# A three-layer transformer stack in one kernel: the first norm's scale vector transposed and applied after the transpose, instead of broadcast

## The chip, the cores and the metric

One core of one Trainium2 chip runs the whole kernel in one launch. TensorE (PE) multiplies, ScalarE (ACT), VectorE (DVE) and GpSimd (POOL) do the rest, SyncE (SP) issues most of the loads over 16 DMA engines. The metric is the device time of one execution in microseconds (us), as the median of several runs.

## What is computed

The input `x` has 256 tokens of 1024 features, in float32. Two blocks follow each other. The first has two layers, each a norm, an attention mixer and a feed-forward part; the second has one layer with a gated feed-forward part ahead of its mixer and one behind. Every matrix product is made in float32 accuracy out of a high and a low part of each operand. What the change touches is the very first step, the norm ahead of the first mixer, whose result is multiplied by the mixer's weights:

```
def rmsnorm(x, g):
    xf = x.astype(jnp.float32)
    y = xf * lax.rsqrt(jnp.mean(xf * xf, axis=-1, keepdims=True) + RMS_EPS)
    return (y * g.astype(jnp.float32)).astype(x.dtype)

hn = rmsnorm(h, mix_norm[layer])        # layer 0: h is x
h = h + moba_nsa_mixer(hn, ...)         # begins with hn @ w_in
```

## The kernel before

The 256 tokens are two token tiles of 128 (index t), the 1024 features eight k tiles of 128. Products want the features on the partitions, so a normed token tile (`xn`, [128 tokens, 1024]) is transposed by TensorE, 128 columns at a time, four k tiles to a PSUM bank. The helper `turn` (L389) does this: four transposes into one bank, then `split` (L385), one ACT copy of [128, 512] into the rounded part `hi` and one DVE subtraction of [128, 512] that leaves the rest, `lo`. Both go to the tile `xx` ([128, 8 k tiles, 512]: `hi` of 256 tokens, then `lo` of 256).

The weights come as a stream of chunks (class `Stream`). SP loads a chunk into `raw`; ACT and DVE split it into `whi` and `wlo` in pieces; `pump` (L96) emits the next piece that is due. The first two chunks are small ([128, 1120], four k tiles of 280 columns each); the first of them is loaded and split in two halves of 560 columns.

`setup` (L523) issues the first loads on SP's queue in this order: `x` of token tile 0 in two halves, the scale vector `mix_norm[0]` broadcast to all 128 partitions (`gain`, L148, by `load_bc`, L144: 128 copies of 4 KB), the identity (part of `cst`), the two halves of the first chunk, `x` of token tile 1, the second chunk, the small tables `rel_bias` and `oh`, the rest of `cst`. It also has PE multiply zeros `WARM` = 4 times, [128, 128] by [128, 384], ahead of anything useful; the trace shows two records for each.

`start_norm` (L583) emits, in this order: the norm of tile 0 (`prenorm`, L430), one split piece, the turn of tile 0 (two banks), one split piece, the norm of tile 1, one split piece (the second chunk). A norm is `squares` (L405, two ACT passes with sums), `ms` on DVE (L422), a power on POOL (L415), and two DVE products `xn = x * r * gain` of [128, 512] (`scaled`, L425). The turn of tile 1 is kept in `late_turn` and emitted later, by `begin` (L315), raised in priority by `soon(300)` over the 300 instructions emitted before it.

`setup`, `start_norm` and `rel_tables` (L561, the table of relative biases, which has one PE product, a DVE copy into S and a trip through memory on POOL's queue) stand inside `tc.manual_schedule()` (L1503). What comes after, from `even` (L598) on, is ordered by the framework's own scheduler. The waits between engines are put in by the framework.

`even` begins with `begin`: for token tile 0, then tile 1, the product with the first two chunks, 8 k tiles by 3 products (hi by hi, hi by lo, lo by hi) of 280 columns, so 24 for each tile. Behind it come products of 256 columns that need `xx` of both token tiles (`projB`, L219; in the trace `ps_p<-xx,whi`).

Of the kernel before, what the change touches and what calls it, by code (L numbers as in the profile page):

```python
# [15 lines left out]
BIG = 1e30  # L16
# [5 lines left out]
WARM = 4  # L22
# [12 lines left out]
class Stream:  # L35
    """The weights in the order of their use: DMA -> raw, raw -> hi (ScalarE) and lo = raw - hi (VectorE)."""
# [26 lines left out]
    def piece(self):  # L63
        """Emits half a chunk's split; False where its buffers or its data aren't due yet."""
        if self.prepped >= len(self.split):
            return False
        j = self.prepped
        c = self.split[j]
        if c.raw is None or (not c.spare and c.ring >= RING and not self.ring[c.ring - RING].done):
            return False  # L70
        K, nc = self.K, self.K.nc
        if c.hi is None:
            if c.spare:
                both = K.t([128, 4096], "T16", 1, F32R)
                c.hi, c.lo = both[:, :2048], both[:, 2048:]
            elif c.n == 128:
                both = K.t([128, 2048], "whi", RING, F32R)
                c.hi, c.lo = (both[:, :256].rearrange("p (k a n) -> p k a n", k=8, a=2)[:, :, i] for i in range(2))
                c.both = both[:, :256].rearrange("p (k n) -> p k n", k=8)
            else:  # L80
                c.hi = K.t([128, 2048], "whi", RING, F32R)
                c.lo = K.t([128, 2048], "wlo", RING, F32R)
        a, b = c.at, (c.n if c.n - c.at <= 1200 else c.at + 1024)
        if not j and not a:
            b = c.n // 2
        if c.n == 128:
            K.split(c.hi, c.lo, c.raw[:, :128].rearrange("p (k n) -> p k n", k=8))
        else:
            K.split(c.hi[:, a:b], c.lo[:, a:b], c.raw[:, a:b])
        c.at = b  # L90
        if b == c.n:
            self.prepped += 1
            self.load()
        return True
# [19 lines left out]
class Kern:  # L114
# [12 lines left out]
    def soon(self, n):  # L127
        """What is emitted inside comes before the n instructions emitted last, where it can."""
        return self.tc.high_priority(offset=n)

    def later(self, inst, than):
        """inst comes after than in their engine's order."""
        self.tc.add_manual_dep(getattr(inst, "ins", inst), getattr(than, "ins", than).name, mybir.DependencyInfo(
            mybir.DependencyClass.NoSync, mybir.DependencyReason.DATA), reason="order")
# [80 lines left out]
    def mmo(self, out, l, r, start):  # L215
        """One start in a bank: later products write or add, column by column, as those stand."""
        self.nc.tensor.matmul(out, l, r, start=start, stop=False, skip_group_check=True)  # L217

    def projB(self, c, f, ps, xx, w=256, quantum=4, one=True):  # L219
        """Features f of chunk c, feature-major: ps[:, :256] = W^T x^T, or the sum of ps's halves where not one."""  # L220
# [15 lines left out]
    def addB(self, ps, dst):  # L236
        """dst = left half + right half of a projB result."""
# [9 lines left out]
    def chunkB(self, xx, evac):  # L247
        """One chunk of 256 features; evac(f, ps)."""
# [13 lines left out]
    def smallB(self, xx, evac):  # L262
        """[128 tokens, 2, 16] product with the chunk of 16 features, for evac, by way of the feature-major
        one: (W_hi | W_lo)^T x_hi and W_hi^T x_lo, whose parts the turn adds."""
# [20 lines left out]
    def projA(self, c, out, xx, k0, nk, n, start, stop, T=(0, 1)):  # L285
        """out[t] ([128 tokens, n]) += x[t] W, nk k tiles from k0."""
# [11 lines left out]
    def chunkA(self, xx, n, evac, ready=None):  # L298
        """Two chunks of 4 k tiles, n columns, token-major; evac(t, ps), once ready()."""
# [15 lines left out]
    def begin(self, xx, items):  # L315
        """The start of a layer, token-major, token tile 0 before tile 1 is there.  items: (n, evac) for n
        columns in two chunks of 4 k tiles, or (256, evac) for a chunk of 256 features; evac(t, ps) may
        return what is to follow once tile 1's products are under way."""
# [29 lines left out]
    def flush(self):  # L348
        """Emits what waits for the next products to be under way."""
# [3 lines left out]
    def feature_major(self, evac, func=AF.Copy, tag="b"):  # L353
        """An item of begin() whose features go to evac(f, ps) as from chunkB."""
# [15 lines left out]
    def down(self, c, acc, hx, k0, start, stop, T=(0, 1)):  # L370
        """acc[t][half] += h[t] W, the two k tiles of c ([2, 1024])."""
# [17 lines left out]
    def turn(self, src, xx, k0, t, n=4, tag="b", than=None):  # L389
        """xx[:, k0:k0+n, token tile t] = hi and lo of the transposed src ([128 tokens, n * 128]); not before  # L390
        the product than."""
# [13 lines left out]
    def squares(self, halves, junk):  # L405
        """Two parts of mean(x^2) of 1024 columns given in two halves"""
# [11 lines left out]
    def rstd(self, halves, junk, eps):  # L418
        """(mean(x^2) + eps)^-1/2 of 1024 columns given in two halves"""
# [19 lines left out]
    def attend(self, jobs):  # L439
        """Causal softmax attention, one job a head: ready(), qk = [(q, k) feature-major] (one or two  # L440
        maps, q times minus its scale), T() = minus the bias with +BIG where masked ([128, 128] for
        query tile 0, [128, 256] for 1), v, O() and col.  Scores, transposes and products with v of
        a head are two and three steps apart."""
# [79 lines left out]
    def setup(self):  # L523
# [13 lines left out]
        self.G0 = self.gain("mix_norm", 0, nc.sync)  # L537
        nc.sync.dma_start(c[:, 0:128], A["cst"][:, 0:128])
        self.ws.load(1)
# [21 lines left out]
    def rel_tables(self):  # L561
        """T[p, h, 255 - j] = -bias_h(128 + p - j), +BIG where that distance is negative."""
# [15 lines left out]
    def back(self, ap):  # L578
        """ap with its last dimension from the end."""
# [3 lines left out]
    def start_norm(self, eps):  # L583
        xx = self.xx = self.t([128, 8, 512], "xx", 2, F32R)
        a = self.prenorm(0, self.G0, eps)
        self.ws.pump(1)
        self.turn(a, xx, 0, 0, 8)
        self.ws.pump(1)
        b = self.prenorm(1, self.G0, eps)
        self.ws.pump(1)  # L590

        def late():
            with self.soon(300):
                self.turn(b, xx, 0, 1, 8, "p")
        self.late_turn = late

# [264 lines left out]
    def early_out(self, F, flag, oT, ks):  # L861
        """First k tiles of an output projection, token tile 0, while attention still runs."""
# [11 lines left out]
    def late_out(self, rest, epi, nlate=2):  # L874
        """The rest of an output projection: rest = (source, k) for each chunk that follows the early ones."""
# [74 lines left out]
    def post_epi(self, f, Gp, G, eps, out=None):  # L950
        """x += f norm(acc) Gp, and its prenorm or the end."""
# [108 lines left out]
    def log1pexp(self, z, n):  # L1060
        """log(1 + e) with e = exp(-|z|), z [128, n]: 2 artanh(t), t = e / (2 + e) <= 1/3, by its series to t^15."""
# [134 lines left out]
    def mixer2(self):  # L1196
# [182 lines left out]
        def ssm_end(g):  # L1379
            """sz is twice z's silu."""  # L1380
# [152 lines left out]
def _cols(w, n):  # L1533
    """[1024, N] -> chunks of n columns, [N / n, 128, 8 * n]"""
# [4 lines left out]
def _halves(w):  # L1539
    """[1024, 512 * m] -> [2 m, 128, 4 * 512]: 512 columns, 4 of the k tiles"""  # L1540
# [4 lines left out]
def _rows(w):  # L1545
    """[K, 1024] -> [K / 256, 128, 2 * 1024]"""
# [86 lines left out]
```

## Time and profile before

| | |
|---|---|
| median of 3 runs | 1233.01 us |
| lowest and highest run | 1232.15 and 1237.44 us |
| profiled execution, first to last instruction (its span) | 1230.5 us |
| profiled execution's own time | the page gives the span alone; the median of the runs lies 2.5 us above it |
| busy: PE, DVE, ACT, POOL | 1204.9, 782.9, 659.3, 122.1 us |
| mean granted TensorE clock | 0.993 of the upper level |
| moved by DMA | 211.32 MB, mean 172 GB/s |

The busy times are those of one execution, and the engines work beside each other. PE is busy for 98% of the span. A wait of another engine counts only where PE waits for it in turn.

### The profile page before, as it was taken

Reading aid. Unit: us, or ns where it says so; the run is one execution under the profiler, and the core shown is the slowest. Engines: PE = TensorE matmul, PEld = TensorE weight load, DVE = VectorE, ACT = ScalarE, POOL = GpSimd, SP = SyncE. Lnnn points to the kernel's source line nnn. Section 1 sums busy time; section 2 is a strip of 40 time slices with the busy share of each in tenths; the row PEclk is TensorE's granted clock in tenths of the full one; section 3 lists DMA queues with packets and bytes.
Section 4 is the critical chain, followed back from the end, with each engine's and each line's share of the span. In section 5 each row is a group of like instructions: output and inputs, shape, how many; then the busy total and the mean of one; then the engine's idle time right before and its main releaser. Section 6 shows DMA issues by size and latency. Waiting matters only on the chain.

```text
span 1230.5 us, 17938 instructions
## 1 busy us (share of the span) xinstructions
PE 1204.9 (98%) x7008; PEld 1035.4 (84%) x7008; DVE 782.9 (64%) x1339; ACT 659.3 (54%) x1209; POOL 122.1 (10%) x182
## 2 busy tenths in 40 slices
PE   8999999999999999999999999999999999999997
PEld 6988888888888888888888988888897778988886
DVE  5566466666755546566676665666788877556564
ACT  5565454545544555454565555565674665555562
POOL 2101000000004330000000100000425120000000
PEclk8999999999999999999999999999999999999999
DMA  8635245555536232655563655562543326455550
GB/s 284 251 120 188 70 154 211 199 181 196 207 121 240 104 137 103 199 195 181 195 221 137 227 176 201 175 238 89 187 172 120 121 86 219 175 178 199 176 201 35
DMA packets 32533, 211.32 MB, mean 172 GB/s; under 512 B 3792, under 2 KB 4592, under 8 KB 8640
## 3 DMA queue, kind: packets, MB, share of 16 engines
q1 hardware_dynamic: 29040, 199.54, 45.5%
q0 software_dynamic: 3120, 10.38, 2.6%
q8 instruction: 55, 0.90, 0.3%
q10 hardware_dynamic: 288, 0.26, 0.1%
q14 instruction: 30, 0.25, 0.1%
HBM read 208.81 MB, written 1.09 MB: 171 GB/s over the span
## 4 chain that ended last, share of the span: by engine, by line
PE 87%; DVE 7%; ACT 2%; issue 2%; POOL 1%; DMA 1%; SPq 0%; POOLq 0%; DVEq 0%; ACTq 0%
PE ps_b L213 40%; PE ps_p L213 26%; PE ps_o L213 15%; DVE wlo L387 3%; PE ps_o L217 3%; PE ps_b L456 1%; PE ps_p L396 1%; PE ps_b L396 1%; ACT whi L386 1%; DVE k L1262 1%; ACT xn L409 1%; DMA S<-in_oh 1%; POOL rs L415 1%; DVE xn L426 1%; DVE x L960 0%
## 5 line engine op out<-in xcount | busy, mean ns | idle before, releaser
L387 DVE TENSOR_TENSOR wlo<-raw,whi 128x1024 fp32r<-128x1024 f32 (+1 forms) x365 | 445.0, 1237 | 236.0 <-ACT whi L386 235.0
L386 ACT ACTIVATE whi<-raw 128x1024 fp32r<-128x1024 f32 (+1 forms) x367 | 377.0, 1048 | 197.9 <-PE ps_p L213 90.6
L213 PE MATMUL ps_b<-xx,whi 128*128 128x512 f32 x1024 | 361.6, 394 | 0.0
L213 PE MATMUL ps_b<-xx,wlo 128*128 128x256 f32 x1024 | 289.1, 282 | 0.0
L213 PEld LDWEIGHTS ps_b<-xx,whi 128*128 128x128 f32 x1024 | 192.3, 188 | 43.9
L213 PEld LDWEIGHTS ps_b<-xx,wlo 128*128 128x128 f32 x1024 | 192.5, 188 | 1.7
L213 PE MATMUL ps_p<-xx,whi 128*128 128x256 f32 (+2 forms) x800 | 148.5, 288 | 1.0 <-DVE fz L1247 0.7
L213 PEld LDWEIGHTS ps_p<-xx,whi 128*128 128x128 f32 (+2 forms) x800 | 121.9, 186 | 7.7 <-issue 5.0
L213 PE MATMUL ps_p<-xx,wlo 128*128 128x256 f32 x384 | 108.6, 283 | 0.0
L213 PE MATMUL ps_b<-whi,xx 128*128 128x256 f32 (+2 forms) x440 | 103.6, 321 | 0.0
L415 POOL TENSOR_TENSOR rs<-ms,mhalf 128x1 f32<-128x1 f32 x22 | 14.9, 675 | 816.9 <-DVE ms L422 816.9
L213 PE MATMUL ps_p<-whi,xx 128*128 128x512 f32 x232 | 83.5, 414 | 1.6 <-DVE xx L387 1.0
L213 PEld LDWEIGHTS ps_b<-whi,xx 128*128 128x128 f32 x440 | 73.2, 189 | 5.3
L213 PEld LDWEIGHTS ps_p<-xx,wlo 128*128 128x128 f32 x384 | 72.7, 189 | 0.2 <-issue 0.2
L213 PE MATMUL ps_p<-whi,q 128*128 128x512 f32 x216 | 71.5, 391 | 0.0
L213 PE MATMUL ps_o<-whi,q 128*128 128x512 f32 x216 | 71.4, 391 | 0.0
L213 PE MATMUL ps_b<-wlo,xx 128*128 128x256 f32 (+2 forms) x220 | 70.5, 321 | 0.3 <-DVE wlo L387 0.2
L241 ACT ACTIVATE tB<-ps_b 128x256 f32<-128x256 f32 x128 | 47.8, 373 | 40.8 <-PE ps_b L213 40.8
L497 ACT ACTIVATE P<-S,nm 128x128 f32<-128x128 f32 x112 | 50.0, 448 | 26.9 <-DVE nm L494 26.6
L213 PE MATMUL ps_p<-whi,k 128*128 128x512 f32 x184 | 61.4, 394 | 0.0
L213 PE MATMUL ps_o<-whi,k 128*128 128x512 f32 x184 | 61.1, 393 | 0.0
L213 PEld LDWEIGHTS ps_p<-whi,xx 128*128 128x128 f32 x232 | 43.4, 188 | 16.9 <-issue 5.6
(317 smaller groups left out, 1775.0 us busy)
## 6 DMA issues: line engine op xcount, KB each, us to landing
raw<-in_w_m SPq DMA_DIRECT2D x64, 1024.0 KB, 4.8
raw<-in_w_s SPq DMA_DIRECT2D x16, 1024.0 KB, 4.7
raw<-in_w_o SPq DMA_DIRECT2D x12, 1024.0 KB, 4.8
raw<-in_w_f1g SPq DMA_DIRECT2D x11, 1024.0 KB, 4.7
raw<-in_w_f1u SPq DMA_DIRECT2D x11, 1024.0 KB, 4.7
raw<-in_w_f1d SPq DMA_DIRECT2D x11, 1024.0 KB, 4.7
raw<-in_w_f2g SPq DMA_DIRECT2D x11, 1024.0 KB, 4.8
raw<-in_w_f2u SPq DMA_DIRECT2D x11, 1024.0 KB, 4.8
```

Of the source, the lines that this page charges most:

```text
L213: self.last_mm = self.nc.tensor.matmul(out, l, r, start=start, stop=stop)
L217: self.nc.tensor.matmul(out, l, r, start=start, stop=False, skip_group_check=True)
L241: nc.scalar.activation(tmp[:m], ps[:m, 256:512], AF.Copy)
L386: self.nc.scalar.activation(hi, src, AF.Copy)
L387: self.nc.vector.tensor_sub(lo, src, hi)
L396: i = self.nc.tensor.transpose(ps[:, k * 128:k * 128 + 128], src[:, (b + k) * 128:(b + k) * 128 + 128], self.ident)
L409: self.nc.scalar.activation(junk[:, h * 512:h * 512 + 512], halves[h], AF.Square, scale=1.0 / 32, accum_out=ss[:, h:h + 1])
L415: self.last_pow = self.nc.gpsimd.tensor_tensor(r, m, self.mhalf, op=OP.pow)
L426: self.nc.vector.scalar_tensor_tensor(dst, src, r, G, op0=OP.mult, op1=OP.mult)
L456: nc.tensor.transpose(b[:, c * 128:c * 128 + 128], P[:, c * 128:c * 128 + 128], self.ident)
L497: nc.scalar.activation(P[:, o:o + w], s[:, o:o + w], AF.Exp, scale=-1.0, bias=nm[:, a:a + 1], accum_out=J["sum"][:, a:a + 1])
L1262: nc.vector.scalar_tensor_tensor(xc[:, f], u[:, f, w:w + 256], cw[:, f, w:w + 1], xc[:, f], op0=OP.mult, op1=OP.add)
```

## The change

- The broadcast load of `mix_norm[0]` goes. In its place SP loads the same 1024 numbers as 8 rows of 128 (`g8`, 4 KB), one place later in the queue, behind the identity. It uses one of the two buffers of the tag `gain`, as the broadcast did.
- `start_norm` first has PE transpose `g8` to [128, 8] and DVE copy that to `gT`: a feature per partition, a column per k tile.
- The norm's scaling (`scale`) multiplies by the token's `r` alone. ACT does the first 512 columns and DVE the other 512.
- The turn works per k tile: after four transposes into one bank, four times an ACT pass over [128, 128] that multiplies by the k tile's column of `gT` and rounds (`hi`), and a DVE pass over the same [128, 128] that multiplies again and subtracts `hi` (`lo`). That holds for both token tiles.
- The two banks of tile 0 are emitted with a split piece of the first chunk between them: bank, piece, bank, piece, norm of tile 1, piece. Before it was piece, bank, bank, piece, norm, piece.
- `WARM` goes from 4 to 3.

All other lines of the diff take away comments.

```diff
-WARM = 4
+WARM = 3
...
         c = self.cst = self.t([128, 1080], "cst")
-        self.G0 = self.gain("mix_norm", 0, nc.sync)
         nc.sync.dma_start(c[:, 0:128], A["cst"][:, 0:128])
+        self.g8 = self.t([128, 1024], "gain", 2)[:8, :128]
+        nc.sync.dma_start(self.g8, A["mix_norm"][0].rearrange("(k p) -> k p", p=128))
         self.ws.load(1)
...
     def start_norm(self, eps):
+        nc = self.nc
         xx = self.xx = self.t([128, 8, 512], "xx", 2, F32R)
-        a = self.prenorm(0, self.G0, eps)
+        gT = self.t([128, 8], "gT")
+        ps = self.bank()
+        nc.tensor.transpose(ps[:, :8], self.g8, self.ident[:8, :8])
+        nc.vector.tensor_copy(gT, ps[:, :8])
+
+        def scale(t):
+            x = self.x[:, t, :]
+            xn = self.t([128, 1024], "xn", 2)
+            r = self.rstd([x[:, s] for s in self.H], xn, eps)
+            nc.scalar.activation(xn[:, :512], x[:, :512], AF.Identity, scale=r)
+            nc.vector.tensor_scalar(xn[:, 512:], x[:, 512:], r, None, op0=OP.mult)
+            return xn
+
+        def turn(xn, t, b, tag):
+            ps = self.bank(tag)
+            for k in range(4):
+                nc.tensor.transpose(ps[:, k * 128:k * 128 + 128], xn[:, (b + k) * 128:(b + k) * 128 + 128],
+                                    self.ident)
+            for k in range(4):
+                p, g = ps[:, k * 128:k * 128 + 128], gT[:, b + k:b + k + 1]
+                hi = xx[:, b + k, t * 128:t * 128 + 128]
+                nc.scalar.activation(hi, p, AF.Identity, scale=g)
+                nc.vector.scalar_tensor_tensor(xx[:, b + k, 256 + t * 128:256 + t * 128 + 128], p, g, hi,
+                                               op0=OP.mult, op1=OP.subtract)
+
+        a = scale(0)
+        turn(a, 0, 0, "b")
         self.ws.pump(1)
-        self.turn(a, xx, 0, 0, 8)
+        turn(a, 0, 4, "b")
         self.ws.pump(1)
-        b = self.prenorm(1, self.G0, eps)
+        b = scale(1)
         self.ws.pump(1)

         def late():
             with self.soon(300):
-                self.turn(b, xx, 0, 1, 8, "p")
+                for k in (0, 4):
+                    turn(b, 1, k, "p")
         self.late_turn = late
```

## Rows read from the trace of the kernel before

**Rows 1.** The page of the kernel before, parts 1 and 4: TensorE's busy time and share of the span, and the shares of the chain that ended last by engine.

```profile
PE 1204.9 (98%) x7008; PEld 1035.4 (84%) x7008; DVE 782.9 (64%) x1339; ACT 659.3 (54%) x1209; POOL 122.1 (10%) x182
...
PE 87%; DVE 7%; ACT 2%; issue 2%; POOL 1%; DMA 1%; SPq 0%; POOLq 0%; DVEq 0%; ACTq 0%
```

**Rows 2.** Windows: the busy time of each engine in four stretches of the span. Columns: stretch in us, its length, busy us (and instructions) of PE, PEld, DVE, ACT and POOL, then the granted TensorE clock (1.00 is the upper level, 0.50 the lower), the DMA share and GB/s.

```profile
22.57:97.00 74.43, 74.43 (x572) 67.22 (x570) 46.28 (x122) 44.82 (x110) 8.62 (x11) 1.00 0.55 190
...
12.00:13.00 1.00, 1.00 (x5) 0.82 (x4) 0.85 (x2) 1.00 (x5) 0.00 (x0) 0.50 0.99 401
...
18.00:19.00 1.00, 1.00 (x8) 1.00 (x8) 0.60 (x2) 1.00 (x2) 0.00 (x0) 0.72 0.91 344
...
394.00:401.00 7.00, 7.00 (x35) 6.84 (x35) 2.10 (x8) 2.55 (x10) 6.99 (x16) 0.51 0.01 4
```

**Rows 3.** Loads of the first 40 us: from the timeline of SP, the fourth load it issues (start, duration); from the DMA view, two loads with KB and us from issue to landing; from the waits, who waited for the broadcast vector (us in total, times, longest).

```profile
2.11 0.43 SPq L538 DMA_DIRECT2D cst<-in_cst  x1
...
gain<-in_mix_norm SPq DMA_DIRECT2D x1, 512.0 KB, 6.7
...
rb<-in_rel_bias SPq DMA_DIRECT2D x1, 2.0 KB, 7.7
...
DVE xn L426 <- DMA gain<-in_mix_norm: 3.3, 1, 3.3
```

**Rows 4.** The timeline of ACT in the start (start us, duration us, engine, line, operation, out<-in, count, and in brackets the idle time before it and what ended it): the first weight split, the second tile's squares, the second chunk's split, the last copy of the second tile.

```profile
9.56 0.67 ACT L386 ACTIVATE whi<-raw 128x560 fp32r<-128x560 f32 x1 [4.57 <-DMA raw<-in_w_ev]
...
11.73 0.62 ACT L409 ACTIVATE xn<-x 128x512 f32<-128x512 f32 x1
...
12.87 0.19 ACT L409 ACTIVATION_READ_ACCUMULATOR xn<-x 128x1 f32 x1
...
12.98 1.14 ACT L386 ACTIVATE whi<-raw 128x1120 fp32r<-128x1120 f32 x1
...
17.91 0.60 ACT L386 ACTIVATE xx<-ps_p 128x512 fp32r<-128x512 f32 x1 [0.49 <-PE ps_p L396]
```

**Rows 5.** The timeline of DVE in the same stretch, with the same columns.

```profile
5.02 0.16 DVE L422 SCALAR_TENSOR_TENSOR ms<-ss 128x1 f32<-128x1 f32 x1 [5.02 <-ACT xn L409]
...
10.26 0.74 DVE L387 TENSOR_TENSOR wlo<-raw,whi 128x560 fp32r<-128x560 f32 x1 [0.33 <-ACT whi L386]
...
13.09 0.16 DVE L422 SCALAR_TENSOR_TENSOR ms<-ss 128x1 f32<-128x1 f32 x1 [0.24 <-ACT xn L409]
...
13.91 1.42 DVE L426 SCALAR_TENSOR_TENSOR xn<-x,rs,gain 128x512 f32<-128x512 f32 x2 [0.67 <-POOL rs L415]
...
15.24 1.32 DVE L387 TENSOR_TENSOR wlo<-raw,whi 128x1120 fp32r<-128x1120 f32 x1
...
18.54 0.69 DVE L387 TENSOR_TENSOR xx<-ps_p,xx 128x512 fp32r<-128x512 f32 x1 [0.40 <-ACT xx L386]
...
19.49 2.36 DVE L387 TENSOR_TENSOR wlo<-raw,whi 128x1024 fp32r<-128x1024 f32 x2
```

**Rows 6.** The timeline of POOL in the same stretch: a memset of a later function and the memset of start-up's last part.

```profile
1.11 0.12 POOL L619 MEMSET kcmp<- 128x30 f32 x1
...
13.83 0.19 POOL L567 MEMSET S<- 16x127 f32 x1
```

**Rows 7.** PE in the start: from its timeline the warm-up, the first transposes and the first product of the next chunk; then, from the chain in order of time (start us, us, what), PE's pieces from the first after the table's load.

```profile
2.28 5.49 PE L213 MATMUL ps_b<-P 128*128 128x384 f32 x8 [2.28 <-ACT P L528]
...
9.32 1.32 PE L396 MATMUL ps_b<-cst,xn 128*128 128x128 f32 x8 [1.56 <-DVE xn L426]
...
22.57 0.40 PE L213 MATMUL ps_p<-xx,whi 128*128 128x256 f32 x2
...
13.46 1.01 PE ps_b L213 x2
...
15.94 0.85 PE ps_p L396 x4
...
17.88 0.47 PE ps_b L213 x2
...
19.91 2.82 PE ps_b L213 x22
```

**Rows 8.** Groups of instructions by line with each shape by itself, over the whole span: busy us, mean ns of one, then the idle time before them and what ended it. These are the nearest rows for operations that the kernel before doesn't have.

```profile
L738 ACT ACTIVATE par<-ps_p 120x128 f32<-120x128 f32 x2 | 0.6, 278 | 1.1 <-PE ps_p L737 1.1
...
L245 ACT ACTIVATE q<-ps_p 128x256 f32<-128x256 f32 x24 | 9.0, 374 | 7.3 <-PE ps_p L213 7.2
...
L1260 ACT ACTIVATE k<-ps_p,par 128x256 f32<-128x256 f32 x10 | 5.6, 563 | 0.0
...
L409 ACT ACTIVATE xn<-x 128x512 f32<-128x512 f32 x32 | 20.0, 627 | 29.1 <-DVE x L931 19.6 <-DVE x L960 6.2 <-DVE x L426 1.9
...
L387 DVE TENSOR_TENSOR whi<-raw,whi 128x128 fp32r<-128x128 f32 x2 | 0.6, 292 | 8.8 <-ACT whi L386 8.8
...
L1448 DVE SCALAR_TENSOR_TENSOR P<-P,r 128x128 f32<-128x128 f32 x8 | 2.8, 349 | 0.1
...
L808 DVE TENSOR_TENSOR mr<-mr,gate 128x8 f32<-128x8 f32 x4 | 0.5, 165 | 0.0
...
L957 DVE SCALAR_TENSOR_TENSOR xn<-ps_p,gain 128x512 f32<-128x512 f32 x6 | 4.1, 685 | 3.7 <-ACT xn L409 3.7
...
L213 PE MATMUL ps_p<-kcmp,q 128*128 128x30 f32 x16 | 2.0, 275 | 0.0
```

## The prediction, made before the changed kernel ran

> **What bounds the kernel now.** I read the page first. TensorE (PE) is busy 98% of the span and holds 87% of the chain that ended last [rows 1]: time is won or lost only where PE waits or runs at its lower clock. Then the windows over the stage that the change touches and what follows it [rows 2]: from 22.57 us to 97 us PE has no idle time at all, and the first product of the next chunk starts at 22.57 [rows 7]. So the change is worth what it does to that moment, its late start being passed on to everything behind. The windows also show the clock: it is at the lower level (0.50 granted) in the 12 to 13 us slice, back at the upper one inside the 18 to 19 us slice (0.72, so at about 18.6), and low once more from 394 to 401 [rows 2]. PE's chain is unbroken from 13.46 [rows 7], so the clock rose after some 5.1 us of unbroken work. A product of 280 columns takes 0.235 us at the lower level and 0.128 at the upper (x2 in 0.47, x22 in 2.82) [rows 7].
>
> Next the wait that the change aims at: VectorE (DVE) idles 3.3 us before the first norm's product until the broadcast scale vector lands, 6.7 us after issue [rows 3]. Last, the engine timelines of the first 22 us. ScalarE (ACT) and DVE run what start_norm emits in the order of emission. The plainest sign is on GpSimd: its memset of S needs nothing, yet runs at 13.83 behind the second power, while memsets from a later function, outside the hand-ordered block, run at 1.11 [rows 6]. I use that order below.
>
> **What is taken away.** The 512 KB broadcast goes and 4 KB comes. The 3.3 us wait goes with it, and what is behind it in SP's queue (weights, second token tile, tables) lands earlier. That saves nothing by itself: the next user of the first weights, ACT's split at 9.56 [rows 4], is now emitted behind the first bank's evacuation, which ends later than that, as follows. Were the 4 KB as slow as the 2 KB of rel_bias (7.7 us to land [rows 3]; issued as the fourth load, at 2.11 [rows 3], so 9.8), the transposed vector would come 3.3 us late; rel_bias sits behind 2.7 MB in the queue (the sizes of the loads ahead of it), the 4 KB behind 0.6 MB, so I take no delay. Two of eight warm-up records go, 1.37 of 5.49 us: PE is free at 6.40, not 7.77 [rows 7].
>
> **A new wait at the head of DVE.** The transpose of the vector and its copy are emitted ahead of the norm. PE reaches that transpose at 6.40; it takes 0.27 (the 128x30 product) and the copy 0.17 (128x8) [rows 8], so DVE is held to about 6.86, and the mean (`ms`), which ran at 5.02 [rows 5], is queued behind it, then the power and both scalings. From `ms` to scaling is 0.82 us (13.09 to 13.91) [rows 5]: 7.7. ACT scales one half in 0.63 [rows 8] plus what a per-partition operand costs: the Identity of 128x256 with two of them takes 0.563 against 0.374 for a plain copy [rows 8], 0.095 each; so 0.72. DVE's half was 0.71 with the gain (1.42 for two [rows 5]) and runs beside it, hidden. PE starts the transposes at 8.5 where before it was 9.32, and four take 0.66 [rows 7]; first evacuation at 9.25. Were DVE to run `ms` first, all of this would come 1.9 us earlier; I keep that as a lower bound.
>
> **The evacuation, the largest term.** Before: per bank one ACT copy and one DVE difference of 128x512, 0.60 and 0.69 [rows 4, 5], bank two under bank one. After: four pairs per bank. An ACT `hi` of 128x128 out of PSUM is 0.278 plain [rows 8], with one operand 0.37. A DVE `lo` is 0.29 plain to 0.35 for the scalar_tensor_tensor with a per-partition scalar [rows 8]. `lo` needs its `hi`. Whether the next `hi` may run beside that `lo`, in the same bank, no row shows; from the nearest rows, wherever ACT and DVE both read one bank, the second waited for the first (L957, whose idle time ended with ACT's squares of the same accumulators [rows 8], though a shared scratch tile may be the reason there). Bounds: beside each other, four pairs cost 1.2 us of ACT; one after the other 4 x (0.37 + 0.35 + 0.05) = 3.1. I take 3.1.
>
> The Trainium skill speaks against the change here: in "PSUM — Partial Sum Buffer", section "PSUM bank collisions raise a hardware error", two engines must not touch the same bank and quadrant at once, reads included, and have to be ordered. By that rule it is the 3.1, never the 1.2; no run here shows it yet.
>
> The chain then, in emission order. Bank one's four pairs: 9.25 to 12.3. ACT's first weight half from 11.9, DVE's to 13.3 (0.67, 0.74 [rows 4, 5]). Bank two's first `lo` waits for that: four pairs end at 15.95. Second weight half on ACT to 16.15. Then the second tile's squares, 1.33 (11.73 to 13.06 [rows 4]): 17.4; they were done at 13.06. Scaling from 18.25 to 18.95; PE's transposes from 19.05, where they were at 15.9 [rows 7]. The second chunk's split behind it: ACT 1.14 to 20.0, DVE 1.32 to 21.3 [rows 4, 5]. The second tile's turn is outside the hand-ordered block, so its two banks may alternate: eight `lo`, done 3.1 later, at 24.4 (before: 18.54 + 0.69 = 19.2 [rows 5]).
>
> PE from 19.05: eight transposes (0.85 for four at the lower level [rows 7]) to 20.75, then 12 products of tile 0 that wait for the second chunk and 24 of tile 1. In the changed kernel PE has had 12 products at most between 10 and 19 us, and in the trace of before the clock fell by 12 after a gap of 1.6 us (7.77 to 9.32 [rows 7]) and a few short ones, so I put it at the lower level, until 5.1 us of unbroken work, 24.15: that is 14 or 15 products at 0.235, and 21 or 22 at 0.128 until 26.9. Against 22.57: +4.3 us. At the upper level throughout, the evacuation binds: 24.4 and the last products, 0.4, so 24.8, +2.2. At the lower throughout, 20.75 + 36 x 0.235 = 29.2, +6.6.
>
> The relative-bias tables hang on DVE's copy into S behind all this; attention, which reads them, starts with the same delay. Nothing else is moved: later gains use the same two buffers, and no load but the vector's changes its place in SP's queue.
>
> **Sum.** The profile's span is 1230.5, the median of the runs 2.5 above it, and I put that on again: 1230.5 + 4.3 + 2.5 = 1237.3, taken as 1237. A measurement of this kernel tells about 0.5% (6.2 us) from no change, so this is within it.
>
> **Rivals.**
> 1. *The pairs overlap.* If ACT may run its next `hi` beside the `lo` (a bank in 1.2, the rest of the chain as above), bank one ends at 10.5, two at 12.3, squares at 14.2, scaling at 15.7, second chunk at 18.1; PE works unbroken from 15.8, is at the upper level from 20.9, and ends at 23.7: +1.1, 1234. At the upper level throughout: 21.3, -1.3. For it: the rows show only pairs that also share data. Against it: not one pair in a bank is seen side by side.
> 2. *The second tile is strictly serial too, slower.* If its banks don't alternate, the eight pairs after 21.3 end at 27.0; if the two halves of the next chunk's split stand between them, as DVE's 2.36 us at 19.49 [rows 5] stand right behind the turn now, 29.4. With 0.4 for the last products: 29.8, +7.2, 1240. It decides from 28.8 on, 6.2 us behind 22.57. For it: DVE waits idle half of each pair, and an in-order engine fills that with a split of 1.18 us. Against it: the turn is emitted with priority over what came before.
> 3. *The clock decides.* The stretch at 394 to 401 [rows 2] is 7 us at half pace, worth 3.4, and hangs on a gap just before; a shift may lose it or make another. With the forecast, one more gives 1240.7, one less 1233.6; with rival 1, one less 1230.7.
> 4. *The change doesn't take the wait away*, the small load being as slow as the large: +3.3 on the forecast, 1240.6.
>
> **How the numbers follow.** Forecast 0.54 (its own range 1235 to 1239.2), rival 1 0.23, rival 2 0.14, rival 3 0.07 (half on each side), rival 4 0.02. Slower by over 0.5% (above 1239.2): rivals 2 and 4 and half of 3, 0.19. Faster (below 1226.8) takes rival 1 at the upper clock and the stretch at 394 lost as well: 0.02, out of rival 1. Same: the rest, 0.79. For the range I leave out one in ten on each side: 1230.5 is rival 1 at its best less a little, 1241 takes in rival 2 and the extra clock stretch.
>
> **What would show it.** In the profile after: no wait for the vector's load; `ms` at about 6.9, not 5.0; the transposes at 8.5; `hi` of one bank starting only when the `lo` before it has ended, 0.77 apart; squares of tile 1 near 16 to 17.4; the 256-column products starting at about 27, not 22.57; the rest as before. It is wrong if the `hi` are 0.3 apart, if `ms` runs at 5.0, if PE stays at the upper level through the first 27 us, or if the order of work behind 30 us is another.

## The result, and the profile after

The changed kernel takes 1240.8 us (median of 6 runs, 1236.18 to 1246.04), the kernel before 1232.62 beside it (6 runs). The ratio is 1.0068 with a 95% interval of 1.0045 to 1.0092: **slower by 0.68%**, 8.2 us, and the interval in microseconds is 5.5 to 11.3. The forecast was 1237.0, within 0.5%.

The page of the profiled execution (part 1; its run took 1242.11) answers to [rows 1]:

```profile
span 1240.3 us, 17963 instructions
...
PE 1210.4 (98%) x7007; PEld 1036.9 (84%) x7007; DVE 783.4 (63%) x1350; ACT 663.4 (53%) x1223; POOL 122.0 (10%) x182
```

The span is 9.9 us longer than before's, PE is 5.5 us longer busy with one row less, DVE and ACT are busy as long as they were within 1% (0.5 and 4.1 us more). So part of the loss is waiting of PE and part is slower products. To place it I used the powers on GpSimd (the `rs` of the norms) as landmarks: they are the same 26 instructions in both kernels. From the timeline of POOL, the third, the seventh, the sixteenth, the seventeenth and the last, first in the kernel before, then in the changed one (start us, duration):

```profile
161.81 0.57 POOL L415 TENSOR_TENSOR rs<-ms,mhalf 128x1 f32<-128x1 f32 x1 [31.86 <-DVE ms L422]
...
480.42 0.56 POOL L415 TENSOR_TENSOR rs<-ms,mhalf 128x1 f32<-128x1 f32 x1 [20.94 <-DVE ms L422]
...
862.56 1.40 POOL L415 TENSOR_TENSOR rs<-ms,mhalf 128x1 f32<-128x1 f32 x1 [2.80 <-DVE ms L422]
...
955.20 0.57 POOL L1390 TENSOR_TENSOR rs<-ss,mhalf 128x1 f32<-128x1 f32 x1 [1.43 <-DVE ss L1388]
...
1225.30 0.55 POOL L415 TENSOR_TENSOR rs<-ms,mhalf 128x1 f32<-128x1 f32 x1 [4.34 <-DVE ms L422]
```

```profile
167.75 0.57 POOL L415 TENSOR_TENSOR rs<-ms,mhalf 128x1 f32<-128x1 f32 x1 [31.93 <-DVE ms L422]
...
488.15 0.56 POOL L415 TENSOR_TENSOR rs<-ms,mhalf 128x1 f32<-128x1 f32 x1 [21.04 <-DVE ms L422]
...
870.33 1.40 POOL L415 TENSOR_TENSOR rs<-ms,mhalf 128x1 f32<-128x1 f32 x1 [2.80 <-DVE ms L422]
...
964.82 0.57 POOL L1421 TENSOR_TENSOR rs<-ss,mhalf 128x1 f32<-128x1 f32 x1 [1.43 <-DVE ss L1419]
...
1235.21 0.55 POOL L415 TENSOR_TENSOR rs<-ms,mhalf 128x1 f32<-128x1 f32 x1 [4.34 <-DVE ms L422]
```

The lag is 5.94 us at 168, 7.73 at 488, 7.77 at 870, 9.62 at 965 and 9.91 at the end. It arises in the start and then in two jumps of about 1.8 us, with almost nothing in between. The windows name the jumps: the granted clock (third figure from the end) is at the lower level for 10.3 us in the start, for 10.4 us from 399.4 and for 3.4 us from 935.4.

```profile
10.40:20.70 10.30, 6.84 (x23) 4.81 (x22) 5.27 (x12) 6.55 (x15) 0.69 (x2) 0.50 0.52 190
20.70:28.00 7.30, 6.17 (x37) 4.89 (x37) 5.65 (x13) 5.60 (x13) 2.08 (x3) 1.00 0.72 228
...
399.40:409.80 10.40, 10.40 (x47) 9.12 (x45) 3.62 (x11) 5.09 (x13) 7.54 (x18) 0.51 0.04 18
935.40:938.80 3.40, 3.40 (x14) 3.11 (x15) 2.84 (x5) 1.33 (x2) 0.92 (x2) 0.50 0.17 72
```

Before had 7 us at 394 [rows 2], 3.4 less, and none near 930; 3.4 us at half pace are worth 1.7, which is each jump. In the start, the timeline of PE:

```profile
6.42 0.27 PE L591 MATMUL ps_b<-cst,gain 8*128 8x8 f32 x1
8.47 1.10 PE L605 MATMUL ps_b<-cst,xn 128*128 128x128 f32 x8 [1.78 <-ACT xn L598]
...
12.49 0.60 PE L213 MATMUL ps_o<-whi,xx 128*128 128x280 f32 x1 [1.36 <-ACT whi L386]
...
25.45 0.80 PE L213 MATMUL ps_b<-whi,xx 128*128 128x280 f32 x2 [0.65 <-DVE xx L611]
...
28.02 0.39 PE L213 MATMUL ps_p<-xx,whi 128*128 128x256 f32 x2
```

The first product of 256 columns, at 22.57 before [rows 7], starts at 28.02: **+5.45**, where +4.3 was forecast. The timeline of DVE shows what PE waited for (line 592 copies the transposed vector, 611 is the `lo` of a pair), and below it one `hi` of a pair from the timeline of ACT:

```profile
6.73 0.17 DVE L592 COPY gT<-ps_b 128x8 f32<-128x8 f32 x1 [6.73 <-PE ps_b L591]
6.81 0.15 DVE L422 SCALAR_TENSOR_TENSOR ms<-ss 128x1 f32<-128x1 f32 x1
...
9.56 0.35 DVE L611 SCALAR_TENSOR_TENSOR xx<-ps_b,gT,xx 128x128 fp32r<-128x128 f32 x1 [1.39 <-ACT xx L610]
10.35 0.35 DVE L611 SCALAR_TENSOR_TENSOR xx<-ps_b,gT,xx 128x128 fp32r<-128x128 f32 x1 [0.43 <-ACT xx L610]
...
21.11 0.60 DVE L611 SCALAR_TENSOR_TENSOR xx<-ps_p,gT,xx 128x128 fp32r<-128x128 f32 x2
...
22.19 1.23 DVE L387 TENSOR_TENSOR wlo<-raw,whi 128x1024 fp32r<-128x1024 f32 x1 [0.16 <-ACT whi L386]
23.39 0.61 DVE L611 SCALAR_TENSOR_TENSOR xx<-ps_p,gT,xx 128x128 fp32r<-128x128 f32 x2
23.92 1.21 DVE L387 TENSOR_TENSOR wlo<-raw,whi 128x1024 fp32r<-128x1024 f32 x1
25.05 0.60 DVE L611 SCALAR_TENSOR_TENSOR xx<-ps_p,gT,xx 128x128 fp32r<-128x128 f32 x2
25.83 0.61 DVE L611 SCALAR_TENSOR_TENSOR xx<-ps_p,gT,xx 128x128 fp32r<-128x128 f32 x2 [0.18 <-ACT xx L610]
```

```profile
9.95 0.37 ACT L610 ACTIVATE xx<-ps_b,gT 128x128 fp32r<-128x128 f32 x1 [0.42 <-DVE xx L611]
```

The mean, ready to run at 5.02 before [rows 5], stands behind the vector's copy; the pairs of a bank follow each other at 0.79 us; and two pieces of the next chunk's weight split, 1.23 and 1.21 us, stand between the pairs of tile 1, whose last `lo` ends at 26.44.

### The profile page after: what moved, and what is told of

It is laid out like the page before. It is cut to its first block, busy times and chain, and to the rows that moved or that the text cites. A ratio compares the mean times of both kernels' runs of the same rounds, so it can differ in the third digit from the quotient of the medians.

```text
span 1240.3 us, 17963 instructions
## 1 busy us (share of the span) xinstructions
PE 1210.4 (98%) x7007; PEld 1036.9 (84%) x7007; DVE 783.4 (63%) x1350; ACT 663.4 (53%) x1223; POOL 122.0 (10%) x182
## 4 chain that ended last, share of the span: by engine, by line
PE 87%; DVE 7%; ACT 2%; issue 2%; POOL 1%; DMA 0%; POOLq 0%; DVEq 0%; ACTq 0%
PE ps_b L213 39%; PE ps_p L213 26%; PE ps_o L213 15%; DVE wlo L387 3%; PE ps_o L217 3%; PE ps_b L456 1%; PE ps_p L396 1%; ACT whi L386 1%; PE ps_b L396 1%; ACT xn L409 1%; DVE k L1293 1%; POOL rs L415 1%; DVE xn L426 1%; DVE x L991 0%; DVE x L962 0%
## 5 line engine op out<-in xcount | busy, mean ns | idle before, releaser
L213 PE MATMUL ps_b<-xx,wlo 128*128 128x256 f32 x1024 | 286.2, 279 | 0.0
```

Of the source, the lines that this page charges most:

```text
L213: self.last_mm = self.nc.tensor.matmul(out, l, r, start=start, stop=stop)
```

## The experiments

**Theory A**: the start is late by three costs of its own, the wait at the head of DVE, the pairs that follow one another in a bank, and the pieces between tile 1's pairs; the delay is passed on. **Rivals** asked in turn whether those costs overlap (B), whether lateness as such costs clock further on (C), whether only the order counts (D), and whether it is the clock in the start and not the chain (E). The first four expectations (e1 to e4) use the letters otherwise: there A is the pairs that wait for each other in a bank, B the mere number of instructions, and C the wait at the head of DVE. Each kernel was timed beside the kernel before (6 to 12 runs, with 6 to 35 of the kernel before). "First product" is the start of the first product of 256 columns, from one profiled execution; "rest" is what is left of the difference of the medians when the shift of that start is taken off.

| kernel | first product | shift | median | before | difference | rest | ratio, 95% |
|---|---|---|---|---|---|---|---|
| before | 22.57 | | | | | | |
| changed | 28.02 | +5.45 | 1240.80 | 1232.62 | +8.2 | 2.7 | 1.0068 [1.0045, 1.0092] |
| changed, again (e9) | 27.94 | +5.37 | 1241.97 | 1232.57 | +9.4 | 4.0 | 1.0070 [1.0049, 1.0092] |
| e1 two banks | 26.24 | +3.67 | 1238.05 | 1232.76 | +5.3 | 1.6 | 1.0050 [1.0033, 1.0067] |
| e2 mean first | 26.00 | +3.43 | 1239.37 | 1232.76 | +6.6 | 3.2 | 1.0052 [1.0033, 1.0072] |
| e7 both | 24.09 | +1.52 | 1235.45 | 1232.57 | +2.9 | 1.4 | 1.0022 [1.0002, 1.0043] |
| e10 tile 1 together | 26.63 | +4.06 | 1240.35 | 1232.57 | +7.8 | 3.7 | 1.0061 [1.0040, 1.0082] |
| e12 changed, 8 warm-ups | 31.96 | +9.39 | 1243.58 | 1232.21 | +11.4 | 2.0 | 1.0089 [1.0069, 1.0108] |
| e11 vector late | 25.99 | +3.42 | 1236.62 | 1232.21 | +4.4 | 1.0 | 1.0035 [1.0016, 1.0053] |
| e3 no vector | 21.52 | -1.05 | 1232.85 | 1232.76 | +0.1 | 1.1 | 0.9995 [0.9978, 1.0012] |
| e4 broadcast by PE | 19.80 | -2.77 | 1231.34 | 1232.76 | -1.4 | 1.4 | 0.9994 [0.9971, 1.0016] |
| e8 before, 8 warm-ups | 20.72 | -1.85 | 1231.39 | 1232.57 | -1.2 | 0.7 | 0.9989 [0.9970, 1.0009] |

**e1, the pairs alternate between two banks.**

```diff
+        def turn2(xn, t, tag):
...
             for k in range(4):
...
+                for b, ps in zip((0, 4), pss):
...
         a = scale(0)
-        turn(a, 0, 0, "b")
+        turn2(a, 0, "b")
         self.ws.pump(1)
-        turn(a, 0, 4, "b")
         self.ws.pump(1)
...
-                for k in (0, 4):
-                    turn(b, 1, k, "p")
+                turn2(b, 1, "p")
```

In `turn2` all eight transposes of a token tile go into two banks first; then, for each k, come the `hi` and `lo` of the one bank and of the other. Both token tiles are turned so.

> The changed kernel with the pairs of a token tile alternating between its two banks (hi of bank one, hi of bank two, then each lo), both split pieces of the first chunk behind them. Nothing is left out. Theory A, the pairs of one bank wait for each other (0.79 us apart in the changed kernel): with a second bank to fill the wait, the eight pairs of tile 0 take about 3.2 us instead of 6.7 (less the 0.7 of the split between), so second-tile scaling at about 15.5 instead of 18.09 and the first 256-column product at 25.5 instead of 28.02; time about 2.5 us under the changed kernel's. Theory B, the cost is that there are more instructions on ACT and DVE, whatever their order: unchanged, 28.0.

The eight pairs of tile 0 in e1, from the timeline of ACT and then from that of DVE:

```profile
9.16 3.16 ACT L614 ACTIVATE xx<-ps_b,gT 128x128 fp32r<-128x128 f32 x8 [0.75 <-PE ps_b L608]
```

```profile
9.56 3.14 DVE L615 SCALAR_TENSOR_TENSOR xx<-ps_b,gT,xx 128x128 fp32r<-128x128 f32 x8 [1.38 <-ACT xx L614]
```

Eight `lo` in 3.14 us, 0.39 each, with no idle time between them: the same instructions, in one bank 0.79 apart. The second power came 2.57 us earlier (14.93 for 17.50), the first product 1.78, at 26.24 for the 25.5 expected: in this execution the last products of tile 1, from 23.90 on, ran at the pace of the lower clock (two in 0.67 us). What is slow is one bank used by both engines in turn; the number of instructions (the B of this expectation) is the same here.

**e2, the vector's transpose behind the mean and the scaling of tile 0.**

```diff
-        ps = self.bank()
-        nc.tensor.transpose(ps[:, :8], self.g8, self.ident[:8, :8])
-        nc.vector.tensor_copy(gT, ps[:, :8])
...
             r = self.rstd([x[:, s] for s in self.H], xn, eps)
+            if not t:
+                ps = self.bank()
+                nc.tensor.transpose(ps[:, :8], self.g8, self.ident[:8, :8])
...
+            if not t:
+                nc.vector.tensor_copy(gT, ps[:, :8])
```

> The changed kernel with the vector's transpose and copy emitted behind tile 0's mean and scaling instead of ahead of the norm. Nothing is left out. Theory C, DVE's wait for the copy delays the norm and all behind it by the same amount: ms at 4.7 instead of 6.81, first evacuation at 7.4 instead of 9.16, and the first 256-column product at 26.3 instead of 28.02. If instead the chain behind is bound by loads or by the second chunk, the evacuation comes earlier and the 256-column products stay at 28.0.

The timeline of DVE in e2:

```profile
4.76 0.16 DVE L422 SCALAR_TENSOR_TENSOR ms<-ss 128x1 f32<-128x1 f32 x1 [4.76 <-ACT xn L409]
5.66 0.49 DVE L600 TENSOR_SCALAR xn<-x,rs 128x512 f32<-128x512 f32 x1 [0.73 <-POOL rs L415]
6.35 0.17 DVE L602 COPY gT<-ps_b 128x8 f32<-128x8 f32 x1 [0.21 <-PE ps_b L598]
7.53 0.35 DVE L614 SCALAR_TENSOR_TENSOR xx<-ps_b,gT,xx 128x128 fp32r<-128x128 f32 x1 [1.01 <-ACT xx L613]
```

The first `lo` runs at 7.53 and not 9.56, and the first product comes 2.02 us earlier (26.00; 26.3 was expected). The wait at the head of DVE was a matter of emission order alone.

**e7, both of these edits** (the diffs of e1 and e2 together).

> The changed kernel with both earlier edits together: the pairs of a token tile alternate between two PSUM banks, and the vector's transpose and copy stand behind tile 0's mean and scaling. Theory A (the start of the changed kernel is late by the wait at the head of VectorE and by pairs that follow one another inside a bank, each on its own): the two gains add, 28.02 - 1.78 - 2.02 = 24.2 us for the first product of 256 columns, a median near 1235.5 us. Rival B (both edits free the same slack, since the second tile or the next chunk's split takes over): no earlier than the better of the two alone, 26.0 us, and a median of 1238 to 1239 us.

24.09, as theory A's sum said (24.2): the two costs lie in one chain and add. The median, 1235.45, is A's too, and still 2.9 us above the kernel before.

**e10, the next chunk's split held behind tile 1's pairs.**

```diff
                     if t:
                         ws.free(c)
-                    ws.pump(2)
+                    if t or self.g8 is None:
+                        ws.pump(2)
...
-            K.split(c.hi[:, a:b], c.lo[:, a:b], c.raw[:, a:b])
+            hl = K.split(c.hi[:, a:b], c.lo[:, a:b], c.raw[:, a:b])
+            if K.pair:
+                for i, j2 in zip(hl, K.pair):
+                    K.later(i, j2)
...
```

The first hunk, in `begin`, emits no split ahead of tile 1's turn; the second puts the first two pieces behind the last pair.

> The changed kernel with tile 1's eight pairs in one piece: the two halves of the next chunk's split, which stood between those pairs on both engines, are held behind the last pair by an order, with no wait added. Theory A (those two pieces, 1.23 and 1.21 us on VectorE, are what made tile 1's turn longer than the forecast): the last lo of tile 1 ends at 24.0 us in the place of 26.44, the first product of 256 columns starts at 26 us if its own weights, split from 24 us on, let it, and the median is near 1238. Rival D (only the order changes: the product of 256 columns then waits for its weights' split): the first product at 27 to 28.5 us and a median as that of the changed kernel, 1239 to 1241.

The timeline of DVE in e10, its last pair and what follows:

```profile
24.44 0.61 DVE L619 SCALAR_TENSOR_TENSOR xx<-ps_p,gT,xx 128x128 fp32r<-128x128 f32 x2 [0.18 <-ACT xx L618]
25.64 4.63 DVE L394 TENSOR_TENSOR wlo<-raw,whi 128x1024 fp32r<-128x1024 f32 x4 [0.59 <-ACT whi L393]
```

The last `lo` ends at 25.05 for 26.44, the first product starts 1.39 earlier, at 26.63: between A's 26 and D's 27. Tile 1's turn began 0.46 us later in this execution (first `lo` at 21.57 for 21.11), so its eight `lo` took 3.48 us for 5.33, 1.85 less. The three gains, 2.02 + 1.78 + 1.39, make 5.2 us, though the third was not run together with the other two. What they are to be measured by is e3 below, the same order with no vector at all: the changed kernel starts 28.02 - 21.52 = 6.5 us behind it, so some 1.3 us of the cost are not traced. The median did not follow (1240.35, which is D's), so the time of one profile and the median of twelve runs part here: the gain is shown for the start alone.

**e12, the changed kernel with eight warm-up products.**

```diff
-WARM = 3
+WARM = 8
```

> The changed kernel with eight warm-up products in the place of three. By the kernel before with eight, they end at 9.37 us (7.09 us for the sixteen rows) in the place of 6.5, and there the lower clock of 12 to 19 us was gone. In the changed kernel the vector's transpose stands behind them, and the mean of tile 0 behind its copy. Theory A (the new wait at the head of VectorE is a chain: what frees TensorE sets the start): everything up to the first product moves by 9.4 - 6.4 = 3.0 us, less what the higher clock gives back on TensorE's part of the chain (some 1.5 us of transposes and products): the first product of 256 columns at 29.5 to 30.5 us in the place of 28.02, a median of 1242 to 1244. Rival E (the changed kernel is held by the lower clock at the start rather than by the chain): the first product at 27 us or earlier and a median of 1237 to 1239.

From the timeline of PE in e12, and then from that of DVE:

```profile
2.28 8.16 PE L213 MATMUL ps_b<-P 128*128 128x384 f32 x16 [2.28 <-ACT P L528]
```

```profile
10.63 0.17 DVE L592 COPY gT<-ps_b 128x8 f32<-128x8 f32 x1 [10.63 <-PE ps_b L591]
10.71 0.15 DVE L422 SCALAR_TENSOR_TENSOR ms<-ss 128x1 f32<-128x1 f32 x1
```

The warm-up ended at 10.4, not 9.4; the copy moved by 3.90 us and the first product by 3.94, to 31.96 (A had 29.5 to 30.5). The clock gave nothing back: the start had its stretch at the lower level all the same. E falls, and the chain from PE's first free moment to the first product is direct.

**e11, the kernel before with its vector loaded late.**

```diff
-        self.G0 = self.gain("mix_norm", 0, nc.sync)
         nc.sync.dma_start(c[:, 0:128], A["cst"][:, 0:128])
         self.ws.load(1)
         nc.sync.dma_start(self.x[:, 1], xv[:, 1])
         self.ws.load(1)
+        self.G0 = self.gain("mix_norm", 0, nc.sync)
```

> The kernel before with the 512 KB broadcast of the vector issued behind both first weight chunks and token tile 1, 1632 KB later on the same queue; no pairs and no transposed vector. It makes the start late by the same kind of wait that the kernel before had (3.26 us on the vector), only longer: at the 403 to 418 GB/s that the start shows, some 4 us more, a first product of 256 columns at 25.5 to 27 us. Theory A (a late start costs its own length, plus about 0.5 us that creeps in during the first layer): a median 3.5 to 4.5 us above the kernel before. Rival C (a start that is late by this much costs 2 to 3 us more further on, in longer or more stretches at the lower clock): a median 5.5 to 7 us above it, with a mean clock lower by 0.002 or more.

A start 3.42 us late with no pair and no transposed vector in it costs 4.4 us: theory A's size. Yet the mean granted clock of its twelve runs was 0.9909 against 0.9935, which C had asked for (how far that counts stands under e9), and the interval of the ratio (2 to 6.5 us) does not shut C out.

**e3, no vector at all**, in the changed kernel's order.

```diff
-        nc.sync.dma_start(self.g8, A["mix_norm"][0].rearrange("(k p) -> k p", p=128))
...
-        nc.tensor.transpose(ps[:, :8], self.g8, self.ident[:8, :8])
-        nc.vector.tensor_copy(gT, ps[:, :8])
...
         def turn(xn, t, b, tag):
...
+            self.turn(xn[:, b * 128:b * 128 + 512], xx, b, t, 4, tag)
```

> The changed kernel without the scale vector: its load, transpose and copy and the multiplication by it are left out (the first norm has no scale), and the turn is the old one, one copy and one difference of 512 columns per bank. Order of the pieces as in the changed kernel. This is what taking away the broadcast could bring at most. Theory A and C together: first evacuation at 7.2, first 256-column product at 20.5 against 22.57 before and 28.02 after, time about 2 us under the kernel before. If the removed broadcast were worth nothing, 22.6.

21.52 for 20.5 to be expected, and a median like that of before. It is not the most that taking away the broadcast can bring, as I had put it. In this order PE runs the product of the tables ahead of the first weights' products, and stands idle for 2.97 us until the table `oh` has landed (timeline of PE in e3):

```profile
10.81 1.03 PE L213 MATMUL ps_b<-S,rb 32*16 32x256 f32 x2 [2.97 <-DMA S<-in_oh]
```

e4, which keeps the vector and the old order, starts 1.72 us earlier still.

**e4, the kernel before with the vector broadcast by TensorE** into two PSUM banks, which the scaling reads.

```diff
-WARM = 4
+WARM = 2
...
-        self.G0 = self.gain("mix_norm", 0, nc.sync)
+        nc.sync.dma_start(self.g1, A["mix_norm"][0:1, :])
...
+        for s in self.H:
+            ps = self.bank("p")
+            self.mm(ps, self.one[:1, :], self.g1[:, s], True, True)
+            G0.append(ps)
```

> The kernel before with the broadcast made by TensorE: one row of 4 KB is loaded, two products with a column of ones put it into two banks on all partitions, and DVE's scaling reads it there; WARM is 2. Nothing is left out; the turn is the old one. If what was lost is the evacuation per k tile, and the late broadcast load was a real wait, this keeps the gain without the price: scaling of tile 0 at 6 instead of 8.52, first 256-column product at 20 to 21 instead of 22.57, time 1.5 to 2.5 us under the kernel before. If the first weights' load binds instead, 22.5.

The first product comes at 19.80, slightly earlier than expected. So the wait for the broadcast, 3.3 us on the trace [rows 3], was worth 2.8 us at the first product in the old order, and 1.05 in the order of e3. Of the 2.8 us the median keeps 1.4, and the interval takes in no change.

**e8, the kernel before with eight warm-up products.**

```diff
-WARM = 4
+WARM = 8
```

> The kernel before with eight warm-up products in the place of four, so that TensorE is free for tile 0's transposes only at 2.28 + 8 x 1.40 = 13.5 us in the place of 9.32; nothing else differs. It is a late start by another cause, without the vector's transpose and without pairs. Theory A (a late start costs its own length and no more; the rest of what the changed kernel lost is the scatter of the stretches at the lower clock): first product of 256 columns at 25.5 to 27 us, and at an equal mean granted clock the run is 3 to 4.2 us longer, a median of 1235.7 to 1237. Rival C (a start that is late by so much brings longer stretches at the lower clock later on, whatever delayed it): the same first product, but a mean clock below that of the kernel before by 0.002 or more and a median of 1238 or more.

It did not make the start late, so it does not tell A from C. The timeline of PE in e8, and then the window from 12 to 19 us:

```profile
2.28 7.09 PE L213 MATMUL ps_b<-P 128*128 128x384 f32 x16 [2.28 <-ACT P L528]
9.20 1.19 PE L396 MATMUL ps_b<-cst,xn 128*128 128x128 f32 x8
```

```profile
12.00:19.00 7.00, 5.93 (x40) 4.74 (x39) 5.99 (x10) 5.42 (x11) 1.24 (x3) 1.00 0.96 369
```

Sixteen rows took 7.09 us, 1.6 more than eight before (5.49 [rows 7]), and end where the vector is scaled anyway. PE has no gap before its transposes, the granted clock stays at the upper level where before it was at 0.50 [rows 2], and the first product comes 1.85 us earlier. The twelve runs bear it out: their mean granted clock is 0.9959, that of 33 of the kernel before 0.9930. My price of 1.40 us for a warm-up product held for the first ones alone.

**e9, the changed kernel again**, unaltered.

> The changed kernel once more, on the same chip and beside the same runs as the others, for its many runs with span and mean granted clock of each. Theory A: at an equal mean clock it stands 5.5 to 6 us above the kernel before (the 5.45 us of the start and what creeps in behind), and its mean clocks scatter over the same values as those of the kernel before; median 1238 to 1240. Rival C: its clocks lie lower on the mean, by 0.002 or more, and the median is 1240 to 1242.

1241.97, above theory A's 1238 to 1240 and in C's range, with the start as in the first profile (27.94). The mean clock of its ten runs is 0.9908, that of 33 of the kernel before 0.9930, a difference of the size that C named. That does not show longer stretches further on, for the mean counts the start as well (window of e9):

```profile
10.00:23.00 13.00, 9.54 (x33) 7.32 (x34) 7.56 (x16) 8.99 (x20) 1.16 (x3) 0.50 0.55 191
```

In this profile the clock is at the lower level from about 9.6 to 23.3 us, 13.7 us for some 6.8 before (from 11.8 to 18.6), and 6.9 us at half pace are 0.0028 of the mean. In e11 the stretch in the start is 3.4 us longer than before, 0.0014 of its 0.0026. A's own test, the time at an equal mean clock, does not decide either. Against the straight line through the 33 runs, six of the ten stand 3.4 to 6.4 us above and four 10.2 to 11.1, and e10's twelve fall into two such groups, 5.5 to 6.2 and 9.0 to 11.2. e10's profiled execution is in its upper group, and its record reads 1.00 where the products go at the lower pace (last section). C is neither shown nor shut out.

The profile settles something else. The clock came back 2.6 us later than in the first one (23.3 for 20.7), and yet the last `lo` of tile 1 and the first product came when they had come there (26.35 for 26.44, 27.94 for 28.02). So tile 1's turn sets the first product of the changed kernel, not the clock in the start.

## Why the prediction was wrong

**Right: the mechanism, and its places up to 19 us.** The wait for the vector's load is gone from the waits. `ms` ran at 6.81 (forecast 6.86), the scalings at 7.69 (7.7), the transposes at 8.47 (8.5), the first pair's `hi` at 9.16 (9.25); pairs stand 0.79 apart (0.77). The squares of tile 1 ended at 17.2 (17.4), its scaling started at 18.09 (18.25). The order of emission, read from two memsets on GpSimd, held in the hand-ordered part. So did the rule against the overlap (rival 1): the Trainium skill's page "PSUM — Partial Sum Buffer", section "PSUM bank collisions raise a hardware error", wants accesses of two engines to one bank ordered, and the trace agrees, each engine's idle time of 0.42 to 0.43 us being ended by the other's half of the pair. The wait is one that the program holds; what two engines would do in one bank without it, no run shows. e1, with two banks, shows the two halves side by side.

**Wrong: the term for tile 1's turn and its tail.** I let the eight `lo` of tile 1 end at 24.4 and gave 0.4 us for the last products. They ended at 26.44, because the two pieces of the next split stood between them: with the pieces held back (e10) the eight took 1.85 us less. That was rival 2's second half, set aside because the turn is emitted with priority, and the priority did not keep them out. The other half of that rival did not come: the two banks did alternate, two `lo` following each other in 0.60 us. And the tail was 1.6 us: the product that waited until 25.45 had fifteen more rows behind it on PE, 2.6 us in all. Together these are 3.2 us.

**Wrong the other way: the clock in the start.** I put PE at the lower level until 24.15; it was back at the upper one at 20.7 (first window above), when PE had worked without idle time for 1.8 us (from 18.86), not for 5.1 as in the kernel before. And it did not matter: in e9 it was back at 23.3, with the same first product. I had PE's products as the path that binds; it is tile 1's turn. With the upper level my own working gives 24.8; 24.8 + 3.2 = 28.0 is what was measured. So +4.3 came near +5.45 by luck, by two errors that partly cancel.

**Wrong: that nothing follows the start.** The sum passed the delay on unchanged. In the profiles the lag grows by 0.5 us in the first layer (5.45 to 5.94), then with the clock: +1.8 near 400 and +1.85 near 935. The 0.5 us are mostly a slower pace of PE, not a wait (window from the first product of 256 columns on, in the changed kernel):

```profile
28.02:102.45 74.43, 74.43 (x569) 67.20 (x568) 45.91 (x122) 43.18 (x109) 7.14 (x10) 1.00 0.52 181
```

The same 74.43 us hold 572 products in the kernel before [rows 2] and in e3, and 569 in e2, e7 and e12, always at the upper clock and without idle time; three products are 0.4 us. The kernels with 569 have the transposed vector; what slows them no run shows. I had the clock as a rival of its own (one more stretch: 1240.7), not as something that comes on top of every other case. How much of the 8.2 us is due to this stays open. In the table the rest is positive for all kernels, 0.7 to 4.0 us, and does not grow with lateness: e12, the latest, has 2.0, e11 1.0, and e3 and e8, which start earlier than before, 1.1 and 0.7. A part common to all rows may come from the 22.57, taken from one execution and set against the medians of many; no run shows it. The changed kernel's 2.7 and 4.0 lie 1 to 2 us above the other kernels' mean of 1.8; the intervals are 2 to 3 us to either side. The start, 5.45 + 0.5 = 5.95 us, is shown, and it lies at the lower end of what was measured (5.5 to 11.3 us, and 6.0 to 11.3 in e9); the other 2 to 3 us are only seen in the profiles as clock stretches, not tied to the change, and their cause stays open.

**The side of the bound.** 6.2 us, 0.5%, was the line that I drew between the same and slower. A forecast of +4 with a start term uncertain by 2 us and a clock that moves a run by 1.8 us at a step was nearer to that line than a chance of 0.79 for "the same" admits.

## What to carry to other kernels

A vector applied per k tile out of PSUM turns one wide evacuation per engine into many small ones that alternate between two engines; put them into two banks by turns, or the pair's full length is paid for every tile (0.79 instead of 0.39 us here). Before a wait is removed by an early small step on another engine, look where that step is emitted: here it stood ahead of the mean that every later step needed, and moving it behind gave back 2 us at the first product. And a wait of 3.3 us on the trace was worth 2.8 us at the first product in one order of the pieces (e4) and 1 us in another (e3), and in the median nothing clear of the noise, so ask what is late next before paying 5 us for it.

## What the runs showed of the hardware

- A longer warm-up cost nothing and kept the granted clock up: in the kernel before, eight products in the place of four filled a gap that was idle anyway, and the stretch at 0.50 from 12 us was gone. In the changed kernel the same eight delayed the chain by 3.9 us and the stretch stayed: it began inside a wait of PE of 2.41 us that ended at 16.40.
- A window's granted clock is not always the pace. In e10 the window from 10 to 20 us says 1.00, yet its products of 280 columns follow each other as in the changed kernel at 0.50. First that window, then PE's timeline in e10, last PE's timeline in the changed kernel:

```profile
10.00:20.00 10.00, 6.38 (x20) 3.82 (x19) 4.85 (x12) 6.25 (x15) 0.69 (x2) 1.00 0.46 162
```

```profile
14.12 0.67 PE L219 MATMUL ps_o<-whi,xx 128*128 128x280 f32 x2
```

```profile
13.67 0.67 PE L213 MATMUL ps_o<-whi,xx 128*128 128x280 f32 x2
```

- The same stretches come and go between kernels that are alike behind the start. One near 926 to 948 (3.4 us, 6.8 in e12) is in eight of the profiles, early and late starts among them, and not in those of before, e2 and e7; e4 has 10.2 us at the lower level near 985, where its lead of 3.05 us turned into a lag of 1.67.
